# Strassen's algorithm for the up projection of the second MLP, in eight of eleven column groups, on one Trainium2 core

## The chip, the cores and the metric

One core of one Trainium2 chip runs the whole program in one launch. TensorE multiplies matrices into PSUM (eight banks of 128 x 512 float32 are in use here), VectorE and ScalarE do the elementwise work, GpSimd (POOL) issues the DMAs that add into their destination, and SyncE (SP) issues the plain loads. The metric is the device time of one execution in microseconds, lower being better; it is stated as the median of several executions.

## The reference

The program is a decoder trunk of two layers over 512 tokens of width 1024 in float32. Layer 0 is an attention mixer (eight forgetting heads, eight stick-breaking heads), layer 1 a gated short convolution. Behind each mixer comes an MLP with a causal convolution of three taps. Only the second of these MLPs is touched here:

```python
def conv_ffn(h, norm_g, w_up, conv_w, w_down):
    xn = rms_norm(h, norm_g)
    u = causal_dwconv(xn @ w_up, conv_w)
    g, val = u[..., :D_FF], u[..., D_FF:]
    return (jax.nn.silu(g) * val) @ w_down
```

`w_up` is 1024 x 5632 (2816 gate columns, then 2816 value columns), `w_down` 2816 x 1024. The result is added to the residual `h`.

## The kernel before

Activations lie in SBUF feature-major: 128 features on the partitions, 512 tokens along the free axis; `h` is eight such tiles. Every float32 product is made of three TensorE products of rounded halves (high·high, high·low, low·high), so each operand needs a high half, written by ScalarE as a rounded copy, and a low half, written by VectorE as the difference. For the activations these are `hs_hi` and `hs_lo`, taken from `h` times the norm's gain; the norm's own row, one factor per token, is not ready then, so it is multiplied in afterwards, on the way out of PSUM. `Norm.scaled` holds work back until that row (`norm.row`) exists; `Norm.spread` (L311) writes it.

Weights come in chunks of 512 KB or less. `want` lists them in the order of use. `load` (L215) issues the transfer into a `raw` tile on SP's queue, ScalarE makes `whi` (L245), VectorE makes `wlo` (L246), and there are three buffers of each. `weights` hands out the next chunk and has the two behind it loaded and halved (`AHEAD = 2`), so the instructions of a chunk stand on ScalarE's and VectorE's queues two chunks ahead of their use. `want_sum` lists a chunk that is a sum of blocks of the weight matrix: the first block is loaded, the others are added in the same tile by accumulating DMAs on POOL's queue (L230).

Each engine executes its instructions in the order in which the program issues them, and waits there for what an instruction needs. That order is the order of the Python calls; `clock`, `spend` and `after` only delay a few pieces of work (the norm's sums and row) by an estimate of TensorE's time.

The second MLP has two parts:

- `up` (L949): 22 pairs of 128 gate columns and 128 value columns. Each pair has two chunks; `project` makes 24 products of 512 tokens for each, into PSUM tags "a" (2 buffers) and "b" (4). `gate` then runs on each accumulator: times the norm's row (y, L954), the three taps (`causal_conv`: one ScalarE copy at L362, two VectorE taps at L365), SiLU (L958), and `product`.
- the down projection in `mlp_last` (L1025), by Strassen's algorithm: the inner dimension in two halves of 11 feature tiles, the tokens and the output columns in two halves each. `product` (L1048) writes four blocks a, b, c, d of the gated activations (11 tiles of 256 tokens each), and `add_to` (L1042) adds a into b and b into c by SBUF-to-SBUF accumulating DMAs. Seven products p1, q5, p7, p6, p2, p3, q4 of six steps (`GROUPS`) follow. The halves of an operand are made one product ahead into two pairs of tiles; the weight sums are built in the tile `chain` (p1, q5's neighbours and so on, L230); the seven results are joined on VectorE with the residuals, which TensorE has transposed to token-major.

## Time and profile before

| what | us |
|---|---|
| median of three executions | 1190.8 (1190.32 to 1191.4) |
| the profiled execution, whole | 1190.44 |
| the profiled execution, span on the core | 1188.7 |
| the first matmul of the second MLP starts | 827.32 |
| its norm row is usable on VectorE | 839.88 |
| the 13th chunk (of 44) starts | 895.55 |
| the down projection starts | 1074.02 |
| the last matmul | 1184.57 |

The profile is one execution. Its page gives busy time by engine, the span in 40 slices, DMA queues, the chain of work that ended last, the costliest groups of instructions and the DMA issues. A row of a group names line, engine, operation and "out<-in" by the program's tile names, with a count, and then busy time and the mean of one in ns. A row in order of time gives start, duration, engine, line, and in brackets the idle time before it with what ended that. A row of a stretch gives its bounds, its length, and then for TensorE, its weight loads, VectorE, ScalarE and POOL the busy time with the number of instructions, then the granted TensorE clock, the share of time for which the 16 DMA engines were busy, and GB/s. A DMA row gives the median time from issue to landing. The engine PE is TensorE, DVE is VectorE, ACT is ScalarE.

### The profile page before, as it was taken

The page shows a single profiled execution, that of the slowest core. Times are in us where ns is not written, and L with a number is a line of the kernel's source. Part 1 is how long each engine was busy: PE and PEld are TensorE (multiplying, and loading weights), DVE is VectorE, ACT ScalarE, POOL GpSimd, SP SyncE. Part 2 cuts the span into 40 slices and gives each one's busy share as a digit, 9 for nine tenths or more (in the row PEclk, how much of TensorE's full clock was granted, in tenths as well). Part 3 has the DMA queues.
Part 4 walks back from the last instruction along what each step waited for, and adds up shares of the span by engine and source line. Part 5 has one row for each costly group of instructions (what it writes and reads, how often), then busy time and mean ns, then how long its engine had stood idle before and what let it go on. Part 6 is the DMA issues. An engine that isn't in the chain of part 4 may idle for free.

```text
span 1188.7 us, 14686 instructions
## 1 busy us (share of the span) xinstructions
PE 1178.9 (99%) x5711; PEld 958.0 (81%) x5711; DVE 800.2 (67%) x1270; ACT 523.6 (44%) x794; POOL 44.6 (4%) x77
## 2 busy tenths in 40 slices
PE   9999999999999999999999999999999999999998
PEld 7887787888888888888888888888888888888886
DVE  5787898968777777763333555555677666669884
ACT  6556676645444444432222222333343333337552
POOL 3000000000000000000000000000000000014110
PEclk9999999999999999999999999999999999999999
DMA  6312121123333333332333323324543433369781
GB/s 190 102 37 71 54 71 55 54 72 89 89 101 94 89 101 95 89 94 85 96 98 106 89 89 102 93 89 125 167 107 89 123 104 106 105 147 199 159 225 60
DMA packets 189462, 122.14 MB, mean 103 GB/s; under 512 B 5228, under 2 KB 175516, under 8 KB 189392
## 3 DMA queue, kind: packets, MB, share of 16 engines
q1 hardware_dynamic: 182112, 106.94, 30.0%
q0 software_dynamic: 7120, 14.19, 6.9%
q8 instruction: 45, 0.74, 0.3%
q14 instruction: 25, 0.20, 0.0%
q10 hardware_dynamic: 160, 0.07, 0.0%
HBM read 116.59 MB, written 2.10 MB: 100 GB/s over the span
## 4 chain that ended last, share of the span: by engine, by line
PE 93%; DVE 4%; ACT 1%; issue 0%; DVEq 0%; ACTq 0%
PE psb L266 14%; PE psb L268 14%; PE psb L267 14%; PE psa L266 11%; PE psa L268 11%; PE psa L267 11%; PE psb L534 3%; PE psb L535 3%; PE psb L536 3%; PE psb L652 1%; PE psa L748 1%; PE psa L534 1%; PE psa L535 1%; PE psa L536 1%; DVE rest L693 1%; DVE wlo L246 1%
## 5 line engine op out<-in xcount | busy, mean ns | idle before, releaser
L245 ACT ACTIVATE whi<-raw 128x1024 fp32r<-128x1024 f32 (+3 forms) x192 | 200.1, 1043 | 321.4 <-PE psb L267 142.5
L246 DVE TENSOR_TENSOR wlo<-raw,whi 128x1024 fp32r<-128x1024 f32 (+3 forms) x192 | 230.5, 1201 | 90.7 <-ACT whi L245 89.2
L266 PE MATMUL psb<-hs_hi,whi 128*128 128x512 f32 x592 | 237.4, 401 | 0.0
L268 PE MATMUL psb<-hs_hi,wlo 128*128 128x512 f32 x592 | 234.0, 395 | 0.0
L267 PE MATMUL psb<-hs_lo,whi 128*128 128x512 f32 x592 | 232.8, 393 | 0.0
L266 PE MATMUL psa<-hs_hi,whi 128*128 128x512 f32 x432 | 171.5, 397 | 0.6 <-ACT whi L245 0.6
L268 PE MATMUL psa<-hs_hi,wlo 128*128 128x512 f32 x432 | 170.8, 395 | 0.3 <-DVE wlo L246 0.2
L267 PE MATMUL psa<-hs_lo,whi 128*128 128x512 f32 x432 | 170.4, 395 | 0.0
L365 DVE SCALAR_TENSOR_TENSOR u<-y,taps,u 128x510 f32<-128x510 f32 (+1 forms) x176 | 131.0, 747 | 3.2 <-ACT u L362 0.4
L268 PEld LDWEIGHTS psb<-hs_hi,wlo 128*128 128x128 f32 x592 | 111.2, 188 | 26.3
L266 PEld LDWEIGHTS psb<-hs_hi,whi 128*128 128x128 f32 x592 | 111.4, 188 | 24.7 <-issue 1.2
L267 PEld LDWEIGHTS psb<-hs_lo,whi 128*128 128x128 f32 x592 | 111.2, 188 | 24.7
L268 PEld LDWEIGHTS psa<-hs_hi,wlo 128*128 128x128 f32 x432 | 81.2, 188 | 20.2 <-DVE wlo L246 1.1
L266 PEld LDWEIGHTS psa<-hs_hi,whi 128*128 128x128 f32 x432 | 81.2, 188 | 19.3 <-ACT whi L245 0.9
L267 PEld LDWEIGHTS psa<-hs_lo,whi 128*128 128x128 f32 x432 | 81.1, 188 | 19.3 <-DVE hs_lo L825 0.4
L954 DVE TENSOR_TENSOR y<-psb,nrow_n 128x512 f32<-128x512 f32 x44 | 30.4, 691 | 81.6 <-PE psb L268 81.6
L958 ACT ACTIVATE u<-u 128x512 f32<-128x512 f32 x44 | 27.8, 632 | 89.9 <-DVE u L365 89.8
L362 ACT ACTIVATE u<-y,taps 128x512 f32<-128x512 f32 x88 | 63.1, 719 | 1.2 <-DVE y L954 1.1
L534 PE MATMUL psb<-whi,hs_hi 128*128 128x256 f32 (+1 forms) x162 | 54.7, 338 | 0.0
L535 PE MATMUL psb<-wlo,hs_hi 128*128 128x256 f32 (+1 forms) x162 | 53.2, 328 | 0.0
L536 PE MATMUL psb<-whi,hs_lo 128*128 128x256 f32 (+1 forms) x162 | 53.0, 327 | 0.0
L954 DVE TENSOR_TENSOR y<-psa,nrow_n 128x512 f32<-128x512 f32 x44 | 30.4, 690 | 21.8 <-PE psa L268 18.6
(293 smaller groups left out, 1773.8 us busy)
## 6 DMA issues: line engine op xcount, KB each, us to landing
raw<-in_ffn_w_up SPq DMA_DIRECT2D x88, 512.0 KB, 3.7
raw<-in_attn_w_in SPq DMA_DIRECT2D x24, 512.0 KB, 4.0
raw<-in_conv_w_in SPq DMA_DIRECT2D x24, 512.0 KB, 3.8
raw<-in_ffn_w_down SPq DMA_DIRECT2D x21, 512.0 KB, 3.6
chain<-in_ffn_w_down POOLq DMA_DIRECT2D x15, 512.0 KB, 8.0
raw<-in_ffn_w_down SPq DMA_DIRECT2D x16, 448.0 KB, 3.2
raw<-in_attn_w_out SPq DMA_DIRECT2D x8, 512.0 KB, 3.6
raw<-in_conv_w_out SPq DMA_DIRECT2D x8, 512.0 KB, 3.5
```

The lines of the kernel that those rows point to most:

```text
L245: return (act.activation(hi[:, at_], raw[:, at_], AF.Copy), dve.tensor_tensor(lo[:, at_], raw[:, at_], f32(hi[:, at_]), op=ALU.subtract))
L246: dve.tensor_tensor(lo[:, at_], raw[:, at_], f32(hi[:, at_]), op=ALU.subtract))
L266: made = [pe.matmul(acc, w[0], rhs[0], start=first, stop=False), pe.matmul(acc, w[0], rhs[1], start=False, stop=False), pe.matmul(acc, w[1 ...
L267: pe.matmul(acc, w[0], rhs[1], start=False, stop=False),
L268: pe.matmul(acc, w[1], rhs[0], start=False, stop=last)]
L362: act.activation(dst, src, AF.Copy, scale=tap(2))
L365: dve.scalar_tensor_tensor(dst[:, d:], src[:, 0:S - d], tap(j), dst[:, d:], op0=ALU.mult, op1=ALU.add)
L534: pe.matmul(acc, lhs[0], w[0], start=first, stop=False)
L535: pe.matmul(acc, lhs[0], w[1], start=False, stop=False)
L536: pe.matmul(acc, lhs[1], w[0], start=False, stop=last)
L954: dve.tensor_tensor(y, acc, norm.row, op=ALU.mult)
L958: act.activation(u[0], u[0], AF.Silu)
```

## The change

Up to the second MLP nothing moves. In the second MLP:

- **The up projection.** The 22 pairs are taken as 11 groups of two. The first three groups (`CLASSIC = 3`, six pairs, 12 chunks) are made as before. The other eight are 2 x 2 block products: 1024 inner features in two halves, 512 tokens in two halves, and the columns in two halves, namely the group's 256 gate columns and its 256 value columns. Strassen's algorithm in Winograd's form makes the four output blocks from seven products (p1, p7, p3, p6, p2, q5, q4), each with an inner dimension of 512, 256 columns and 256 tokens: 24 matmuls of 256 columns in `seven`.
- **Operands.** `prepare`, called in two halves at j = 0 and j = 2 of the classic pairs, multiplies `h` by gain and norm row, forms the sums and makes the high and low halves of the seven operands (`forms`), which are kept for all groups.
- **Weights of a group.** The blocks (0,0) into X, (0,1) into Y, (1,0) into W and (1,1) into Z are loaded by SP. Sums: (1,1) is added to Y by POOL, X to Y by VectorE, (0,1) to X by POOL, (1,0) to Y by POOL. Halves are taken in between, for p1, p7, p6, p2, q5, q4 and (one group later) p3.
- **PSUM.** A group uses three banks, A, T and R. Products that enter the same output block are summed in one bank; R starts as the negative of A, copied by ScalarE, so that its matmuls add to what is there.
- **`slot(g, s)`** issues the product s of group g and then the other engines' work that stands behind it: the weights of later products, and the joins, taps, SiLU and product of the group before, now 2 x 512 wide on some engines.
- **`Blocks`** keeps the gated activations in one layout of 22 x 512 in three tiles, with a into b added by two POOL DMAs.
- **The last stage.** The order of the products becomes p1, p7, p6, p2, q5, q4, p3; `operand` makes an operand's halves two steps ahead and remakes the blocks in place for the next product; sums of products are built up in the PSUM banks A, T, R, so that fewer joins are left; the chain tiles and buffers are others.
- Pools: `hs_hi` and `hs_lo` become the tiles `hs_a`, `hs_b`; the norm's tiles get a pool `own`; the pool `work` is closed before the second MLP.

```diff
+CLASSIC = 3
...
-    hs_hi = const.tile([P, ND, S], F32R, tag="hs_hi", name="hs_hi")
-    hs_lo = const.tile([P, ND, S], F32R, tag="hs_lo", name="hs_lo")
+    hs_a = hsp.tile([P, 12, S], F32R, tag="hs_a", name="hs_a")
+    hs_b = hsp.tile([P, 4, S], F32R, tag="hs_b", name="hs_b")
...
-    HF, GROUPS, chain = NF // 2, ((0, 2), (2, 2), (4, 2), (6, 2), (8, 2), (10, 1)), []
+    HF, HT = NF // 2, S // 2
+    GROUPS = ((0, 2), (2, 2), (4, 2), (6, 1), (7, 2), (9, 2))
...
-    want_ffn(1)
-    want_last()
+    want_ffn(1, 2 * CLASSIC)
...
+    class Blocks:
...
+        def product(self, j, n, g, u):
...
+            to = self.at(j, n)
+            plus, minus = (LEFT, RIGHT) if j < HF else (RIGHT, LEFT)
+            dve.tensor_tensor(to[:, :, plus], g[:, :, plus], u[:, :, plus], op=ALU.mult)
+            dve.scalar_tensor_tensor(to[:, :, minus], g[:, :, minus], -1.0, u[:, :, minus], op0=ALU.mult, op1=ALU.mult)
+            for k0, k1 in ((0, HEAD), (HEAD, HF)):
+                if j + n == k1:
+                    nc.gpsimd.dma_start(self.block("b", k0, k1 - k0), self.block("a", k0, k1 - k0), accum_op=ALU.add)
+
+    def seven(acc, w, x, fresh, last=True):
+        for i in range(2):
+            to, c = acc[:, i * HT:(i + 1) * HT], slice(i * P, (i + 1) * P)
+            for k in range(4):
+                for t, (a, b) in enumerate(((0, 0), (0, 1), (1, 0))):
+                    pe.matmul(
+                        to, w[a][:, k, c], x[b][:, k, :], start=fresh and i + k + t == 0,
+                        stop=i == 1 and k == 3 and t == 2, skip_group_check=not fresh)
...
+        def prepare(half):
+            k0 = 2 * half
...
+            for x, f in ((x0, k0), (x1, k0 + 4)):
+                for i in range(2):
+                    dve.scalar_tensor_tensor(x[:, i, :], h[:, f + i, :], gain_of(norm.base, f + i), norm.row, op0=ALU.mult, op1=ALU.mult)
...
+            form("p1", x0[:, :, LEFT])
+            dve.tensor_tensor(s0, x0[:, :, LEFT], x0[:, :, RIGHT], op=ALU.subtract)
+            form("p7", s0)
...
+        def load_pair(g):
+            s = st[g] = {}
+            s["X"], s["Y"] = (mp.tile([P, 4, 2 * P], F32, tag=t, name=f"{t}{layer}{g}", bufs=2) for t in "XY")
+            nc.sync.dma_start(s["X"], block_of(g, 0, 0))
+            nc.sync.dma_start(s["Y"], block_of(g, 0, 1))
...
+        def add_block(g, n, kh, half):
+            nc.gpsimd.dma_start(st[g][n], block_of(g, kh, half), accum_op=ALU.add)
...
+        def slot(g, s):
+            on, was, soon = g in groups, g - 1 in groups, g + 1 in groups
+            form, n, fresh = (("p1", "A", True), ("p7", "T", True), ("p3", "R", False), ("p6", "R", False), ("p2", "A", False),
+                              ("q5", "R", False), ("q4", "T", False))[s]
+            if s == 2:
+                if was:
+                    product(g - 1, form, n, fresh)
+            elif on:
+                product(g, form, n, fresh)
+            p, c = g - 1, st.get(g)
+            if s == 0:
+                if was:
+                    weights_of(p, "p3", "Z")
+                    join(p, "yg", st[p]["T"], st[p]["Xs"])
+                if on:
+                    dve.tensor_tensor(c["Y"], c["Y"], c["X"], op=ALU.add)
+                    add_block(g, "X", 0, 1)
+                    load_one(g, "W", 1, 0)
+                if soon:
+                    load_pair(g + 1)
+            elif s == 1:
+                if on:
+                    act.activation(bank_of(g, "R"), c["A"], AF.Copy, scale=-1.0)
+                    weights_of(g, "p6", "Y")
+                if soon:
+                    add_block(g + 1, "Y", 1, 1)
+                if was:
+                    conv(p, 0, 0)
+            elif s == 2:
+                if on:
+                    kept(g, "P7s", c["T"])
+                    add_block(g, "Y", 1, 0)
+                    weights_of(g, "p2", "W")
+                if was:
+                    conv(p, 0, 1)
+            elif s == 3:
+                if was:
+                    to_wide(p, "yv", LEFT, st[p]["R"])
+                if on:
+                    weights_of(g, "q5", "X")
+                if was:
+                    act.activation(wides[p]["ug"], wides[p]["ug"], AF.Silu)
+                    conv(p, 1, 0)
+            elif s == 4:
+                if on:
+                    kept(g, "Xs", c["R"])
+                    weights_of(g, "q4", "Y")
+                if was:
+                    conv(p, 1, 1)
+            elif s == 5:
+                if was:
+                    blocks.product(2 * p, 2, wides[p]["ug"], wides[p]["uv"])
+                if on:
+                    load_one(g, "Z", 1, 1)
+                    open_wides(g)
+                    to_wide(g, "yg", LEFT, c["A"])
+                if soon:
+                    weights_of(g + 1, "p1", "X")
+            else:
+                if on:
+                    join(g, "yv", c["R"], c["P7s"])
+                if soon:
+                    weights_of(g + 1, "p7", "Y")
...
+            if j == 0:
+                norm.scaled(lambda: prepare(0))
+            if j == 2:
+                norm.scaled(lambda: prepare(1))
+            if j == 2 * CLASSIC - 2:
+                load_pair(base)
+                add_block(base, "Y", 1, 1)
...
+        PHASES = ("p1", "p7", "p6", "p2", "q5", "q4", "p3")
...
+        def operand(i):
...
+            halves_to(t[:, 0, 0:nk, :], t[:, 1, 0:nk, :], blocks.block(name, k0, nk), sign)
+            a, b, c, d = (blocks.block(n, k0, nk) for n in "abcd") if p in (1, 2, 3) else (None,) * 4
+            if p == 1:
+                dve.tensor_tensor(b, b, c, op=ALU.add)
+            elif p == 2:
+                dve.tensor_tensor(a, b, a, op=ALU.subtract)
+            elif p == 3:
+                dve.tensor_tensor(b, b, d, op=ALU.add)
...
+        A, T, R = ([] for _ in range(3))
+        home = {"p1": (A, "a", True), "p7": (T, "b", True), "p6": (R, "b", False), "p2": (A, None, False), "q5": (R, None, False),
+                "p3": (R, None, False), "q4": (T, None, False)}
```

More of the change, by code (lines that the diff above doesn't have):

```diff
@@ L283, in __init__ @@
             self.row, self.held = None, []
-            self.acc = work.tile([P, S], F32, tag="y", name=f"nacc_{name}") if name != "n0" else None
+            self.acc = own.tile([P, S], F32, tag="nrow", name=f"nacc_{name}", bufs=1) if name != "n0" else None
         def feed(self, f, src):
@@ L311, in spread @@
         def spread(self):
-            self.row = work.tile([P, S], F32, tag="nrow", name=f"nrow_{self.name}", bufs=1)
+            self.row = own.tile([P, S], F32, tag="nrow", name=f"nrow_{self.name}", bufs=1)
             t = bank("c")
@@ L397, in trunk, with want_ffn @@
     want_out_last()
-    def want_ffn(layer):
-        for j in range(NF):
+    def want_ffn(layer, pairs=NF):
+        for j in range(pairs):
             want(ffn_w_up[layer], 0, 8, j * P, P)
@@ L521, in values @@
                 w = ws[k // 4]
[L522 removed]
+                mm3_rhs(acc[:, 0:n], [t[:, tok] for t in hs(k)], (w[0][:, k % 4, :], w[1][:, k % 4, :]), k == 0, k == ND - 1)
                 spend(0.33)
```

327 lines of the change are left out of this document (214 added, 113 removed).

## The prediction

> **What bounds the kernel now.** I read the page's first two parts and the chain of work, then busy time by stretches, then order of time on single engines.
>
> ```profile
> span 1188.7 us, 14686 instructions
> PE 1178.9 (99%) x5711; PEld 958.0 (81%) x5711; DVE 800.2 (67%) x1270; ACT 523.6 (44%) x794; POOL 44.6 (4%) x77
> PEclk9999999999999999999999999999999999999999
> PE 93%; DVE 4%; ACT 1%; issue 0%; DVEq 0%; ACTq 0%
> ```
>
> TensorE is busy throughout, at full clock, and carries 93% of the chain. The stretches of the second MLP (columns: us, then each engine's busy time with its count, clock, DMA share, GB/s):
>
> ```profile
> 900.00:922.33 22.33, 22.33 (x98) 18.06 (x97) 15.72 (x23) 8.88 (x13) 0.00 (x0) 1.00 0.33 95
> 839.80:895.50 55.70, 55.70 (x241) 45.02 (x240) 40.79 (x58) 23.19 (x33) 0.95 (x1) 1.00 0.40 113
> 895.50:1074.00 178.50, 178.50 (x769) 144.23 (x769) 123.79 (x172) 69.26 (x92) 9.51 (x9) 1.00 0.44 112
> 1074.00:1188.70 114.70, 110.96 (x495) 89.72 (x493) 86.44 (x114) 59.60 (x82) 21.89 (x19) 0.99 0.70 162
> ```
>
> The 178.5 us hold 768 matmuls of 512 columns, eight groups of 96 (the edges count one or two more): 232.5 ns each, 22.3 us a group, no gap. A weight chunk (24) takes 5.58 us. VectorE is busy 69% here, so it has room that the change can use up.
>
> The profiled execution took 1190.4 us, its span plus 1.7; the median of the three runs is 1190.8, so the sum below stands for both. About 0.2% (2.4 us) is what a measurement of this kernel can tell from no change.
>
> **Part 1: TensorE's work.** A group becomes seven products of 24 matmuls, 168 of 256 columns. The kernel has such matmuls in the attention values; here 13 in a row from 72.85 on:
>
> ```profile
> 72.85 0.28 PE L535 MATMUL psb<-wlo,hs_hi 128*128 128x256 f32 x1
> ...
> 74.39 0.28 PE L536 MATMUL psb<-whi,hs_lo 128*128 128x256 f32 x1
> ```
>
> 13 steps in 1.54 us: 118 ns start to start, weight loads hidden. A product is 2.83 us, a group 19.8 instead of 22.3. If TensorE stayed the bound, eight groups would save 20 us.
>
> **Part 2: the first six pairs (still classic) carry the preparation.** Each half of prepare puts on VectorE 4 scalings, 4 sums and 7 low halves, all 512 wide. Prices:
>
> ```profile
> 839.88 0.69 DVE L954 TENSOR_TENSOR y<-psa,nrow_n 128x512 f32<-128x512 f32 x1 [2.18 <-ACT nrow_n L316]
> 840.49 0.68 DVE L954 TENSOR_TENSOR y<-psb,nrow_n 128x512 f32<-128x512 f32 x1
> 841.09 1.22 DVE L246 TENSOR_TENSOR wlo<-raw,whi 128x1024 fp32r<-128x1024 f32 x1
> 842.22 2.73 DVE L365 SCALAR_TENSOR_TENSOR u<-y,taps,u 128x511 f32<-128x511 f32 x4
> 850.92 0.39 PE L266 MATMUL psa<-hs_hi,whi 128*128 128x512 f32 x1
> ```
>
> Start to start, instructions overlap a little: 512 wide 0.61 us, weights' low half 1.13, tap 0.68. The norm row arrives at 839.9; the fifth chunk's product is due at 850.92. As the changed kernel is built, that chunk's low half stands behind 4 scalings (0.68), 11 operations of 0.61, both y (0.61), 4 taps (0.68) and itself (1.22 to its end): 2.7+6.7+1.2+2.7+1.2 = 14.5, so 854.5. TensorE waits 3.6 us where it waited none. From there to the ninth chunk's low half stand the second half of prepare (2.7+6.7), 4 low halves (4.5), 4 y (2.4), 7 taps (4.8) and 4 products of 256 (0.42 by the row below, some 0.34 start to start: 1.4), 22.5 us, against 4 x 5.58 = 22.3 of TensorE. In ScalarE's order the ninth chunk's high half, which waits until TensorE frees a buffer, stands ahead of prepare's high halves, so VectorE waits there about 1.7: TensorE waits 1.9 more. Sum +5.5; between 3.6 (the second hidden) and 8 (every high half waited for). Then VectorE has 13 us of work in 22, and the backlog is gone before the first Strassen product.
>
> ```profile
> L1052 DVE TENSOR_TENSOR blk_a<-u,u 128x256 f32<-128x256 f32 x11 | 4.7, 426 | 0.4
> L362 ACT ACTIVATE u<-y,taps 128x512 f32<-128x512 f32 x88 | 63.1, 719 | 1.2 <-DVE y L954 1.1
> L316 ACT ACTIVATE nrow_n<-psc 128x512 f32<-128x512 f32 x3 | 1.8, 598 | 12.0 <-PE psc L315 12.0
> raw<-in_ffn_w_up SPq DMA_DIRECT2D x88, 512.0 KB, 3.7
> ```
>
> On SP's queue the last classic chunk's load now stands behind the first X and Y loads, which wait for prepare to let go of their buffers (about 876); it lands 3.7 later, at 880, wanted at 884: 0. The operands also take prepare's results from h, so the norm's row is waited for no longer than by the first y.
>
> The Trainium skill ("TensorE: Matmul & The Clock Gate", Part 1) has TensorE's clock halve after an idle window of about 3.4 us. The first wait is about that long; by that rule up to 1.7 us would be added. No gap of this trace tests it (clock 1.00 in every stretch), and the sum goes without.
>
> **Part 3: the loop of the Strassen groups.** ScalarE's load per group (7 high halves of 1.06, 5 copies of PSUM of 0.6, 4 tap copies of 0.72, one SiLU of about 1) is 14.3 us: cover enough. VectorE: 7 low halves and Y+X (8 x 1.13), 8 taps (5.4), 2 joins and 2 products of 512 (4 x 0.61) = 16.9 us of 19.8. That alone fits. But its order is fixed, and one wait lies in it. p6's low half must be done with Y before POOL may add the fourth block to Y; when that lands, ScalarE makes q4's high half, VectorE its low half, and everything of VectorE behind that (the next p1, p7, p6) queues. From q4's low half to the end of p6's, VectorE runs: five of 1.13 (q4, p1, p7, Y+X, p3), four taps (2.7), two products and two joins (2.4), p6 1.22: 12.0. Around it:
>
> ```profile
> 1063.94 1.23 DVE L246 TENSOR_TENSOR wlo<-chain,whi 128x1024 fp32r<-128x1024 f32 x1 [0.17 <-ACT whi L245]
> 1065.47 1.20 POOL L230 DMA_DIRECT2D chain<-in_ffn_w_down x1 [0.44 <-DVE wlo L246]
> 1103.41 0.90 POOL L230 DMA_DIRECT2D chain<-in_ffn_w_down x1 [0.74 <-DVE wlo L246]
> 816.10 1.06 ACT L245 ACTIVATE whi<-raw 128x1024 fp32r<-128x1024 f32 x1 [3.38 <-PE psb L267]
> ```
>
> 0.3 us from the low half's end (1065.17) to the add's issue, then the landing L, then about 0.1 and 1.06 on ScalarE. So a group takes 13.5 + L, if that is over 19.8: the loop leaves TensorE's bound at L = 6.3. L of single adds of 512 KB, by stretches about one issue each (1122:1124 nothing near it; 1052:1054 one load beside it; 1063:1065 an add 3 us before; 1065:1067 its second row, an add 1.6 us before):
>
> ```profile
> chain<-in_ffn_w_down POOLq DMA_DIRECT2D x1, 512.0 KB, 5.8
> ...
> raw<-in_ffn_w_down POOLq DMA_DIRECT2D x1, 512.0 KB, 6.5
> ...
> raw<-in_ffn_w_down POOLq DMA_DIRECT2D x1, 512.0 KB, 7.1
> chain<-in_ffn_w_down POOLq DMA_DIRECT2D x1, 512.0 KB, 8.0
> ```
>
> Those have 256 pieces of 2 KB; the new blocks have 512 of 1 KB. POOL's instruction took 0.90 for 128 pieces and 1.20 for 256, so 0.6 more. In the loop X's add is issued 4.9 us before Y's, and the load of Z runs beside it: between the 6.5 and the 7.1, 6.8, plus 0.6 is L = 7.4. Ends: 5.8+0.6 = 6.4 and 8.0+0.6+0.7 (the second load) = 9.3. Then a group takes 20.9; TensorE waits 1.1 us at q4, and saves 1.4 a group, not 2.5.
>
> The first group has no p3 and no backlog: 6 products and the next p1 (19.8), p6's halves (1.06+1.22), 0.3+L+1.16, so q4's low half of the second group starts 23.6+L = 31.0 after the first product. Six more rounds of 20.9 are 125.4; then q4's low half, a tap, an operand, two products and the down projection's first low half, 4.9. Two adds inside SBUF for the blocks stand in POOL's queue ahead of X's and Y's once each: 1.5. Sum 162.8 for what took 178.5: -15.7.
>
> What else queues there: POOL issues the next group's (1,1) add ahead of X's. It waits for Y's load, issued after q4's low half (1.3 into the round) and landed 3.7 later, so it is out at 5.1, before X's add can go (7.4). X's add lands at 14.8; q5's halves and three taps behind it end at 19, before Y's landing at 12.4+7.4 = 19.8. Only if X took 2 us more would it be late next.
>
> **Part 4: the last stage.** Its 462 matmuls stay 512 wide. Added: the last group's p3, 24 x 118 ns = +2.8. VectorE's work from the first to the seventh step (18 us: operands, p3's halves, joins and taps of the last group) equals TensorE's 18.2, so it costs at most 0.5. POOL's queue is the risk: q5's adds stand ahead of p6's, nine whole blocks from the stage's start.
>
> ```profile
> 1120.00:1140.00 20.00, 20.00 (x88) 16.22 (x87) 16.24 (x21) 12.27 (x17) 6.95 (x6) 1.00 0.86 146
> ```
>
> Those 20 us at a DMA share of 0.86 hold five adds of 512 KB, one of half that and one load: 17.2 us of all 16 engines. The stretch from 900 has four loads at 0.33 of 22.33, so 1.8 a load, and an add takes 15.4/5.5 = 2.8. Nine are 25.2, two loads among them 3.7, and p6's own first block 5.8: it lands some 34.7 us in, wanted at 32.7: +2 (nothing, if the loads come later; 6, if POOL's waits hold two adds up). With the 0.5, +2.5. The joins that go away, by the sums in PSUM, lay beside TensorE: 0. The tail behind the last matmul is the same.
>
> **Sum:** 5.5 - 15.7 + 2.8 + 2.5 = -4.9: 1185.5 us.
>
> **Rivals.**
> TensorE stays the bound (adds land within 6.3 us): 55 products x 2.83 = 155.7 instead of 162.8, so -4.9-7.1 = -12: 1178.4. For it: 5.8 alone. Against: 7.1 with an add before it, and smaller pieces. The Trainium skill's fit ("DMA: Bandwidth & Descriptors", Anatomy of one DMA), 2.0 us plus bytes over 436 GB/s, gives 3.2 us for 512 KB as an estimate, generation being small, and would bring this case; the trace disagrees, with 5.8 at best.
>
> The add's wait decides against the change: L at its upper end, 9.3, makes a group 22.8, longer than the classic 22.3, and the sum 7 x 1.9 = 13.3 worse: +8.4, 1198.8. Place: q4's low half on VectorE. It decides from L = 8.1 on, where the sum is 0. For it: 8.0 median of the chain's adds, three adds and four loads a group; against: the adds are 5 to 7 us apart, and the 8.0 belong to adds closer than 3.
>
> Narrow matmuls don't keep 118 ns over whole stages, so the change doesn't do what it says: at 133 a group costs 22.3 as before. Against: the row above. At 133 throughout, with parts 2 and 4: +8, 1198.
>
> **How the numbers follow.** Forecast 48%, TensorE-bound 15%, late adds 33%, slow narrow matmuls 4%. The forecast's own range, L from 6.5 to 8.1, is 1179 to 1190. Faster by over 0.2% is L under 7.75: 33 of the 48, and the 15: 0.48. Within 0.2%: 13 of the 48, 2 of the late: 0.15. Slower: 0.37. The range to 80%: 1177 (TensorE-bound, less of part 4) to 1201 (late adds, and 2 us of parts 2 and 4).
>
> **What would show it.** Narrow matmuls 118 ns apart within a product. A wait of 3 to 4 us of TensorE at the fifth chunk, on VectorE's wlo. In each group, a wait of about 1 us at q4's first low-half matmul, on VectorE's wlo, which waited for ScalarE's whi, which waited for the DMA into Y; the period 20.9; Y's add landing 7.4 after its issue. If VectorE shows no wait at q4, the TensorE-bound case holds; if TensorE waits over 2.5 us a group, the late adds do. If TensorE waits at another product, or VectorE's instructions are longer than before, part 3 is wrong in its mechanism.

## The result and the profile after

The changed kernel takes 1198.62 us (median; 1197.68 to 1203.78) against 1190.67 for the kernel before: a ratio of 1.0075, 95% interval 1.0056 to 1.0094. It is slower by 0.75%, where 1185.5 was forecast. Its executions spread over 6 us, those of the kernel before over 1.1.

From the page of the changed kernel:

```profile
span 1195.9 us, 16031 instructions
PE 1169.0 (98%) x6287; PEld 978.8 (82%) x6287; DVE 831.0 (69%) x1292; ACT 572.6 (48%) x859; POOL 74.8 (6%) x98
...
PEclk9999999999999999999999999999999999989999
...
PE 84%; DVE 8%; DMA 5%; ACT 2%; issue 1%; SPq 0%; DVEq 0%; ACTq 0%; POOL 0%; POOLq 0%
```

TensorE is busy 9.9 us less than before. The smaller products alone promise some 17 (20 in the groups, less 2.8 for the last group's p3); the half clock, told of below, takes back 5.4 of them. The span is even 7.2 us longer: TensorE's share of the chain fell from 93% to 84%, DMA appears with 5%. By stretches (classic pairs, Strassen groups, last stage; then three single groups; columns as in the prediction):

```profile
828.80:900.07 71.27, 69.78 (x309) 56.26 (x308) 62.60 (x102) 33.13 (x47) 3.62 (x3) 1.00 0.45 119
900.07:1075.77 175.70, 162.78 (x1321) 162.06 (x1320) 133.88 (x159) 104.41 (x134) 33.91 (x27) 0.96 0.87 185
1075.77:1195.90 120.13, 114.53 (x512) 91.75 (x510) 91.28 (x123) 67.11 (x95) 24.36 (x21) 1.00 0.69 158
...
937.24:964.21 26.97, 21.56 (x170) 21.35 (x169) 17.74 (x21) 13.24 (x17) 4.32 (x4) 0.94 0.86 165
1008.07:1028.13 20.06, 20.06 (x170) 20.02 (x169) 17.09 (x21) 13.48 (x17) 3.48 (x3) 1.00 0.86 184
1048.09:1075.77 27.68, 22.48 (x170) 22.28 (x169) 18.58 (x23) 15.11 (x21) 6.19 (x5) 0.88 0.92 227
```

Against the stretches of before, the classic pairs take 3.0 us more (71.27 for 68.23, from 827.32 to 895.55), the groups 2.8 less (175.70 for 178.5) and the last stage 5.4 more (120.13 for 114.7). About 1.0 us of the 3.0 is work that only changed its place: eight transposes, which the kernel before makes in its last stage, stand among the classic pairs as built. The second MLP starts 1.5 us later (828.80 for 827.32), though nothing ahead of it was changed.

Four of the eight groups take 19.9 to 20.1 us and the first, which has no p3, 17.1, all with TensorE never idle. The other three have a wait each: 5.7, 2.6 and 5.5 us, counted from the start of one matmul to the start of the next. The first of them, on TensorE and then on ScalarE:

```profile
951.32 0.28 PE L1065 MATMUL psa<-p_hi,wlo_p 128*128 128x256 f32 x1
957.01 0.58 PE L1065 MATMUL psb<-q_hi,whi_q 128*128 128x256 f32 x1 [5.41 <-ACT Xs L1160]
```

```profile
951.10 1.06 ACT L1017 ACTIVATE whi_q<-X 128x1024 fp32r<-128x1024 f32 x1 [5.56 <-DMA X<-in_ffn_w_up]
952.06 0.58 ACT L1152 ACTIVATE yv<-psb 128x512 f32<-128x512 f32 x1
952.68 1.33 ACT L370 ACTIVATE uv<-yv,taps 128x512 f32<-128x512 f32 x2
955.42 1.06 ACT L1017 ACTIVATE whi_q<-Y 128x1024 fp32r<-128x1024 f32 x1 [1.41 <-DMA Y<-in_ffn_w_up]
956.38 0.58 ACT L1160 ACTIVATE Xs<-psb 128x512 f32<-128x512 f32 x1
```

The product that waits is q5. It adds to bank R, and before it may, ScalarE must copy R out (Xs). An engine's order was said above to be that of the Python calls. Here it is not: the text of `slot` has Xs ahead of q4's high half, but as built Xs stands behind it on ScalarE, and q4's high half waits for the fourth block's landing in Y. So that landing holds up q5, one product earlier than the prediction had it. X's own add is late here too: its high half starts at 951.10, so q5 would have waited nearly 2 us in any case (1.8 in the run with Xs first, below). What landed when, from single issues of the changed kernel (the add inside SBUF; X's add beside it; Y's fourth block in an undisturbed group; the last group's, with two of the last stage's loads):

```profile
head<-head POOLq DMA_DIRECT2D x1, 896.0 KB, 9.6
...
X<-in_ffn_w_up POOLq DMA_DIRECT2D x1, 512.0 KB, 12.2
...
Y<-in_ffn_w_up POOLq DMA_DIRECT2D x1, 512.0 KB, 6.0
...
p_hi_chain<-in_ffn_w_down SPq DMA_DIRECT2D x1, 512.0 KB, 10.6
Y<-in_ffn_w_up POOLq DMA_DIRECT2D x1, 512.0 KB, 11.7
p_lo_chain<-in_ffn_w_down SPq DMA_DIRECT2D x1, 512.0 KB, 12.3
```

Behind each of the three waits TensorE ran at half its clock (narrow matmuls 213 ns apart instead of 118), for 3.2, 3.4 and 5.1 us:

```profile
957.01:960.20 3.19, 3.19 (x15) 3.19 (x16) 3.16 (x5) 1.39 (x2) 0.00 (x0) 0.50 0.40 111
1001.00:1004.40 3.40, 3.40 (x18) 3.40 (x18) 3.37 (x5) 1.14 (x2) 0.00 (x0) 0.52 0.52 148
1067.71:1072.80 5.09, 5.09 (x24) 5.09 (x25) 4.32 (x6) 3.24 (x6) 0.94 (x2) 0.50 1.04 196
```

That costs 1.5, 1.6 and 2.3 us: 5.4 in all, beside 13.4 of waits (what is left when the matmuls' usual distance is taken off).

### The profile page after: what moved, and what is told of

Its sections match the earlier page's. It is cut to its first block, busy times and chain, and to the rows that moved or that the text cites. A ratio compares the mean times of both kernels' runs of the same rounds, so it can differ in the third digit from the quotient of the medians.

```text
span 1195.9 us, 16031 instructions
## 1 busy us (share of the span) xinstructions
PE 1169.0 (98%) x6287; PEld 978.8 (82%) x6287; DVE 831.0 (69%) x1292; ACT 572.6 (48%) x859; POOL 74.8 (6%) x98
## 4 chain that ended last, share of the span: by engine, by line
PE 84%; DVE 8%; DMA 5%; ACT 2%; issue 1%; SPq 0%; DVEq 0%; ACTq 0%; POOL 0%; POOLq 0%
PE psb L270 11%; PE psb L272 11%; PE psb L271 11%; PE psa L272 8%; PE psb L1065 8%; PE psa L271 8%; PE psa L270 8%; PE psb L1371 4%; PE psa L1065 3%; PE psa L1371 2%; DMA Y<-in_ffn_w_up 2%; PE psb L641 1%; PE psa L737 1%; DMA q_hi_chain<-in_ffn_w_down 1%; DVE wlo L250 1%
## 5 line engine op out<-in xcount | busy, mean ns | idle before, releaser
L270 PE MATMUL psb<-hs_a,whi 128*128 128x512 f32 x464 | 186.4, 402 | 0.0
L272 PE MATMUL psb<-hs_a,wlo 128*128 128x512 f32 x464 | 184.1, 397 | 0.0
L272 PE MATMUL psa<-hs_a,wlo 128*128 128x512 f32 x304 | 121.2, 399 | 1.7 <-DVE wlo L250 1.6
L270 PE MATMUL psa<-hs_a,whi 128*128 128x512 f32 x304 | 120.2, 395 | 1.3 <-ACT whi L249 1.3
L270 PEld LDWEIGHTS psb<-hs_a,whi 128*128 128x128 f32 x464 | 87.6, 189 | 19.9 <-issue 1.2
L272 PEld LDWEIGHTS psb<-hs_a,wlo 128*128 128x128 f32 x464 | 87.1, 188 | 20.1
L271 PE MATMUL psb<-hs_b,whi 128*128 128x512 f32 x232 | 91.7, 395 | 0.0
L271 PE MATMUL psb<-hs_a,whi 128*128 128x512 f32 x232 | 91.7, 395 | 0.0
L1371 PE MATMUL psb<-whi,act 128*128 128x512 f32 x220 | 70.5, 398 | 0.7 <-ACT whi L249 0.6
L373 DVE SCALAR_TENSOR_TENSOR u<-y,taps,u 128x511 f32<-128x511 f32 (+1 forms) x88 | 65.5, 748 | 1.8 <-ACT u L370 0.4
L271 PE MATMUL psa<-hs_b,whi 128*128 128x512 f32 x152 | 60.2, 396 | 0.0
L271 PE MATMUL psa<-hs_a,whi 128*128 128x512 f32 x152 | 60.1, 396 | 0.0
L1065 PE MATMUL psb<-q_hi,whi_q 128*128 128x256 f32 x128 | 39.1, 305 | 12.9 <-ACT Xs L1160 12.9
```

What stands on the lines that cost most here:

```text
L270: made = [pe.matmul(acc, w[0], rhs[0], start=first, stop=False), pe.matmul(acc, w[0], rhs[1], start=False, stop=False), pe.matmul(acc, w[1 ...
L271: pe.matmul(acc, w[0], rhs[1], start=False, stop=False),
L272: pe.matmul(acc, w[1], rhs[0], start=False, stop=last)]
L373: dve.scalar_tensor_tensor(dst[:, d:], src[:, 0:S - d], tap(j), dst[:, d:], op0=ALU.mult, op1=ALU.add)
L1065: pe.matmul(to, w[a][:, k, c], x[b][:, k, :], start=fresh and i + k + t == 0, stop=i == 1 and k == 3 and t == 2, skip_group_check=not fresh)
L1371: pe.matmul(acc[tb], acts[i][:, a, k, tok], w[b][:, k, :], start=fresh and k0 + k + t == 0, stop=k0 + k == HF - 1 and t == 2, skip_group_c ...
```

## The experiments

Every run is compared with the kernel before on the same chip; "the changed kernel" is 1198.6 throughout.

### Where the long waits come from

**The add of a to b moved from POOL's transfers to VectorE.**

```diff
-                if j + n == k1:
-                    nc.gpsimd.dma_start(self.block("b", k0, k1 - k0), self.block("a", k0, k1 - k0), accum_op=ALU.add)
+            if HEAD <= j + n <= HF:
+                k0 = 0 if j + n == HEAD else j
+                b, a = self.block("b", k0, j + n - k0), self.block("a", k0, j + n - k0)
+                dve.tensor_tensor(b, b, a, op=ALU.add)
```

> VectorE adds block a to block b (one addition of 1792 columns in the fourth Strassen group's time, then up to 512 columns a group) in place of the two adding transfers inside SBUF. Theory (shared DMA): the first two long waits of TensorE at q5 (5.7 and 2.6 us) come from these two transfers, beside which the adds into X and Y land 9 to 12 us after their issue where they take 6 to 8 otherwise. Then both waits go, with the 1.5 and 1.6 us of half clock behind them, and only the last group's wait stays: about 10.9 us less than the changed kernel, 1187.5. Rival (the loop is at its edge and lands late by chance): waits of the same sum remain in the loop, 1196 to 1202.

Measured: 1196.31 us, ratio 1.0050 (1.0035 to 1.0065). The two waits shrank from 5.7 and 2.6 to 1.0 and 1.3 us, but others of 3.5 and 1.9 came in groups that had none, and the last group's stayed (5.9). Sum and time are the rival's, nearly; but the waits at the two places that the theory named shrank by 6.0 us, which chance alone doesn't explain. Two things changed at once here: the transfers went, and VectorE got more work.

**The same add left out**, to part the transfers from VectorE's added work.

> The changed kernel without the two transfers that add block a to block b inside SBUF, and with nothing in their place: this part of the computation is left out. It parts the two things that e1 changed together, the transfers taken away and the work put on VectorE. If e1's new waits (3.5 us in the fourth Strassen group, 1.3 and 1.9 us in two others) came from the loop of 13.5 + L itself, which the first long wait had hidden by giving the adds a head start, they are here too: 3 to 6 us of waits in the loop ahead of the last group, 1194 to 1197. If they came from VectorE's added work, no group but the last waits more than 0.5 us: 1187 to 1189.

Measured: 1191.78 us, ratio 1.0008 (0.9999 to 1.0018), so the two transfers cost 6.8 us of the changed kernel. The time lies between the two ranges that were named. Waits of 0.6, 2.1 and 1.5 us remain ahead of the last group; the 3.5 us of the run before is gone, so it came of VectorE's added work. The remaining ones follow the reckoned loop of 13.5 + L. Six groups of this run together, then two of them alone, and the landings of the fourth block in these two:

```profile
916.98:1040.79 123.81, 120.52 (x1010) 119.85 (x1009) 103.74 (x125) 79.96 (x102) 21.83 (x17) 1.00 0.83 179
...
977.48:999.47 21.99, 20.21 (x170) 20.01 (x169) 17.31 (x21) 13.24 (x17) 4.70 (x4) 1.00 0.78 168
1020.84:1040.79 19.95, 19.95 (x170) 19.95 (x169) 17.37 (x21) 13.36 (x17) 2.77 (x3) 1.00 0.85 185
```

```profile
Y<-in_ffn_w_up POOLq DMA_DIRECT2D x1, 512.0 KB, 7.8
...
Y<-in_ffn_w_up POOLq DMA_DIRECT2D x1, 512.0 KB, 6.0
```

With L = 7.8 the loop gives 21.3, measured 22.0; with 6.0 it gives 19.5, and TensorE's 19.95 bounds. Over the six L averages 6.8, which gives 20.3; they took 123.81/6 = 20.6.

**One more such transfer.**

```diff
+        spare = mp.tile([P, 4, HT], F32, tag="spare", name="spare_sum")
+        pool.memset(spare, 0.0)
...
+                    if g == 8:
+                        nc.gpsimd.dma_start(spare, blocks.block("c", 0, 4), accum_op=ALU.add)
```

> One more adding transfer inside SBUF (512 KB, from block c into a tile that nothing reads) is issued on POOL's queue in group 8's slot q5, a group whose successor shows no wait; the output is the same. Shared DMA: in the group after it the adds into X and Y land 2 to 5 us later, and q5 there waits 2 to 3 us, with some 1.6 us of half clock behind: 4 us longer than the changed kernel, about 1202. Rival (chance): no wait comes in at that place, within 1 us of the changed kernel.

Measured: 1199.91 us, ratio 1.0082 (1.0067 to 1.0097). A wait of 1.6 us came in at the named place (2 to 3 were expected), with no half clock behind it; but one of 1.5 came also a group earlier, and the time lies within the changed kernel's spread. The direction fits, and alone it would settle nothing.

**The last group: the last stage's loads held back.**

```diff
                 if fresh:
-                    nc.sync.dma_start(v, src)
+                    issued = nc.sync.dma_start(v, src)
+                    if i >= held_from[0] + 4:
+                        tc.add_manual_dep(issued.ins, gate_at[NF // 2 - 1].ins.name, mybir.DependencyInfo(
+                            mybir.DependencyClass.Sync, mybir.DependencyReason.DATA), reason="hold")
```

> The loads of the last stage, from its fifth chunk on, are held back until ScalarE makes the last Strassen group's q4 high half. Shared DMA: the last group's wait at q5 (5.2 us, with 2.2 us of half clock) comes from the seven loads that SP issues into freed buffers beside the last adds; it falls under 1 us. The first sums of the last stage then land later and give back 0 to 3 us: 1191.5 to 1195. Rival: the add into Y is late for another reason (it is 4.6 us behind X's on POOL's queue), and the wait stays at 4 us or more: 1197 or longer.

Measured: 1202.64 us, ratio 1.0107 (1.0092 to 1.0122). The last group's wait is gone altogether, and its fourth block lands after 6.1 us, so the loads beside it were the cause:

```profile
Y<-in_ffn_w_up POOLq DMA_DIRECT2D x1, 512.0 KB, 6.1
```

But the last stage now waits 3.0 us at 1089 and 7.3 at 1107, each with half clock behind: the held loads were needed. Right on the cause, wrong on the price of the cure.

**The order on ScalarE.**

```diff
-                    kept(g, "Xs", c["R"])
-                    weights_of(g, "q4", "Y")
+                    copied = kept(g, "Xs", c["R"])
+                    behind(weights_of(g, "q4", "Y"), copied)
```

> ScalarE's copy Xs of bank R (which must be taken before q5 adds to that bank) is put ahead of q4's high half in ScalarE's order; nothing else changes. Theory (order on ScalarE): q5 waits because Xs stands behind q4's high half, which waits for the fourth block's add into Y. With Xs first q5 waits only for X's halves, and the add into Y has one product (2.8 us) more: of the three waits (5.7, 2.6, 5.5 us, with 5.3 us of half clock) some 1 us at q5 of the first and 1 to 2 us at q4 of the first and third remain: 1185 to 1188. Rival (q5 waits for its own weights): the waits stay within 1 us, 1197 to 1201.

Measured: 1197.44 us, ratio 1.0061 (1.0044 to 1.0077): 1.2 less, where the changed kernel's own executions spread over 6. The three waits shrank (5.7 to 1.8, 2.6 to none), but q5 waited in other groups (3.2, 1.9, 1.0 us): Xs still stands behind X's high half and three copies, and X's add now went out 0.8 to 1.9 us behind the next group's add into Y (2.2 to 3.7 before) and took 8.4 to 10.6 us, and most of the last group's wait only moved to q4 (2.4 and 1.0 us there, 1.3 left at q5). The order says which product waits, not how long the landings take.

### Taking the landing out of the loop

**The fourth block added by VectorE.** It is the block (1,0), which lies in SBUF as W.

```diff
-                    add_block(g, "Y", 1, 0)
                     weights_of(g, "p2", "W")
+                    dve.tensor_tensor(c["Y"], c["Y"], c["W"], op=ALU.add)
```

> The fourth block of a group, which POOL added to Y by a transfer, is already in SBUF as W: VectorE adds W to Y instead (1.1 us a group), so no landing lies any more between p6's low half and q4's high half. The adds inside SBUF stay. Theory (loop with a landing in it): the waits in the loop were this landing L, in the loop that the prediction reckoned at 13.5 + L a group, made longer by whatever else the DMA engines did. Then no group waits more than 1 us at q5 or q4, the half-clock stretches go, and eight groups take about 157 us: 1198.6 - 13.0 - 5.3 = 1180.5, between 1179 and 1184. Rival (the landing into X is the next limit): q5 waits 1 to 3 us in two or more groups on X's halves, 1185 to 1190. Rival (VectorE becomes the bound at 18.0 us of 19.8): waits on VectorE's low halves in every group, 1186 or more.

Measured: 1189.56 us, ratio 0.9994 (0.9985 to 1.0004), 9 us less than the changed kernel and 9 more than expected. Groups, then last stage, of this run:

```profile
899.89:1062.21 162.32, 159.32 (x1321) 158.43 (x1320) 140.18 (x165) 103.69 (x134) 23.15 (x19) 0.99 0.73 169
1062.21:1188.10 125.89, 117.24 (x512) 93.69 (x510) 92.93 (x125) 66.82 (x95) 24.85 (x22) 0.97 0.69 158
```

The groups gave 13.4 us of the 18 or so that were expected: q5 still waited 2.35 us, with half clock behind, and 0.7 and 0.8 us in two other groups. There X's landing came late, and Xs stands behind X's high half on ScalarE, with four more instructions between. The time lies in the first rival's range, but only in part for its reason: the last stage took back 5.8 (125.89 for 120.13). In it p6 now waits for a weight sum:

```profile
1101.00 0.49 PE L1371 MATMUL psb<-whi,act 128*128 128x512 f32 x1 [4.13 <-ACT whi L249]
1102.26 0.79 PE L1371 MATMUL psb<-wlo,act 128*128 128x512 f32 x1 [0.76 <-DVE wlo L250]
```

The shorter loop brings the stage forward, but not its sums: those start when buffers come free and then take their time on the DMA engines.

**Both adds on VectorE.** The edits of the first run and of the one above together.

> As the run before, and block a is added to b by VectorE too, so that of POOL's transfers in a group only the second and the third block's adds are left. Shared DMA: X's adds land within 6 to 7.5 us in every group, and the time is that of the run before or up to 2 us less: 1179 to 1182. VectorE as the bound: in the groups with the added 1.9 or 0.6 us TensorE waits by about that, 2 to 4 us more than the run before.

Measured: 1193.02 us, ratio 1.0023 (1.0013 to 1.0033): 3.5 us more than the run before, as the second case had it. VectorE, with some 17.6 of 20 us a group (141.11 over eight in a row below), has little room. The large addition stands in its order ahead of Y+X, and behind it Y+X began 3.5 us later than in the run before (940.00 for 936.52), and with it X's add:

```profile
932.79 2.02 DVE L1058 TENSOR_TENSOR head<-head 128x1792 f32<-128x1792 f32 x1
```

So the wait at that q5 stayed (2.55 us), though the transfer beside it was gone, and the last group waited 2.8.

**The preparation one pair later**, on top of the fourth block's edit.

```diff
-            if j == 0:
+            if j == 1:
                 norm.scaled(lambda: prepare(0))
-            if j == 2:
+            if j == 3:
                 norm.scaled(lambda: prepare(1))
```

> As the first run of this call, with the two halves of the operands' preparation put one classic pair later (j = 1 and j = 3 for 0 and 2). The wait of 1.65 us at the fifth chunk (and 0.5 at the ninth) is taken to be VectorE's queue of preparation work right behind the norm's row. Then these waits go or fall under 0.5 us together, and 1 to 2 us less than the first run of this call is measured, 1179. Rival: the same work is late one pair later, or the first Strassen products wait for their weights, whose tiles the preparation lets go later: a wait of 1 to 4 us at the seventh to the 13th chunk, 1180 to 1184.

Measured: 1188.68 us, ratio 0.9983 (0.9973 to 0.9992). The waits of 1.65 and 0.5 us are gone, as expected, and the first Strassen product starts 3.0 us earlier (896.89 for 899.89; 1.0 of it is the eight transposes, back in the last stage). Only 0.9 arrived at the end:

```profile
896.89:1062.92 166.03, 160.13 (x1321) 159.28 (x1320) 140.77 (x167) 104.09 (x135) 24.14 (x19) 0.98 0.73 165
```

The groups took 3.7 us more (166.03 for 162.32): the wait of 2.35 us at q5 grew to 4.5, and the half clock behind it lasted twice as long. X's add went out 2.3 us earlier there but took 12.1 us, for 10.7 in the run before; why is not shown. The last stage took 1.9 less (123.98 for 125.89), still with a wait of 4.4 us ahead of p6.

### The order of POOL's transfers

**q5's adds behind p6's**, on top of the run above.

```diff
+                    adds[i] = nc.gpsimd.dma_start(v, src, accum_op=ALU.add)
+                    if i in after_add:
+                        behind(adds[i], adds[after_add[i]])
...
+        for g in range(6):
+            after_add[at_first + 6 * PHASES.index("q5") + g] = at_first + 6 * PHASES.index("p6") + 5
```

> As e7, and in the last stage q5's six adds are put behind p6's last add on POOL's queue; before, four to six of them stood ahead of p6's adds, which are wanted 31 us earlier. Theory (order of POOL's queue): the wait of 4.4 us at p6's first steps (1097.5 in e7) and the 2 us of half clock behind it come from this order, and they are why the last stage grew when the loop ahead of it became shorter. Then the wait falls under 1 us, and 5 to 6 us less than e7 is measured: 1183. Rival (the DMA engines themselves are the limit there: 12 sums are wanted within 31 us whatever their order): the wait stays at 3 us or more, or moves to p7 or q5, 1187 to 1190.

Measured: 1184.70 us, ratio 0.9955 (0.9940 to 0.9970), 4.0 less (5 to 6 were expected). POOL's queue of the run before, where X, Y and two of the p tiles are q5's sums, and then of this one:

```profile
1079.62 1.20 POOL L234 DMA_DIRECT2D q_hi_chain<-in_ffn_w_down  x1 [3.32 <-DMA q_hi_chain<-in_ffn_w_down]
1080.35 2.64 POOL L234 DMA_DIRECT2D Y_chain<-in_ffn_w_down  x2
...
1093.84 1.20 POOL L234 DMA_DIRECT2D q_lo_chain<-in_ffn_w_down  x1 [0.77 <-DVE wlo L250]
```

```profile
1092.48 1.20 POOL L235 DMA_DIRECT2D q_lo_chain<-in_ffn_w_down  x1 [0.93 <-DVE wlo L253]
1093.21 2.95 POOL L235 DMA_DIRECT2D X_chain<-in_ffn_w_down  x2
```

The wait at p6 is gone. 2.4 us came instead at p2, whose plain loads took 8 to 11 us beside the twelve adds that now went out together.

**Xs first, and the add of a to b in smaller pieces**, on top of that.

```diff
-            for k0, k1 in ((0, HEAD), (HEAD, HF)):
+            for k0, k1 in ((0, 6), (6, HEAD), (HEAD, HF)):
```

> As e8, with Xs ahead of q4's high half on ScalarE, and the adding transfer of block a into b cut so that its first six tiles go right behind the classic pairs and one tile later. Theory: with the large transfer out of the second Strassen group's time X's add there lands in about 7 us, and q5 waits for its own operands alone; the waits of 4.5 and 1.2 us in the loop fall under 1 us together, with 2 us of half clock: 5 to 7 us less than e8, 1176 to 1179. Rival: the first Strassen group, which has three adds of its own, takes the wait over, 1180 to 1183.

Measured: 1186.51 us, ratio 0.9967 (0.9954 to 0.9979): 1.8 us more, a miss. The large add's wait moved a group forward (2.6 us), and waits of 0.6 to 1.5 us stand in five others, where the run before had two. X and Y were loaded 2 to 4 us later, counted from the group's first product, and their two adds went out closer together and landed later. That q4's halves, now behind Xs, let go of Y later is the likely reason; it was not tried apart.

**What is wanted first goes first**, on the last kernel but one (without Xs first and the smaller pieces).

```diff
-                    add_block(g + 1, "Y", 1, 1)
+                    behind(add_block(g + 1, "Y", 1, 1), c["added"])
...
+                    if i in after_low:
+                        tc.add_manual_dep(adds[i].ins, lows[after_low[i]].ins.name, mybir.DependencyInfo(
+                            mybir.DependencyClass.Sync, mybir.DependencyReason.DATA), reason="hold")
...
+        for g in range(6):
+            after_low[at_first + 6 * PHASES.index("q4") + g] = at_first + 6 * PHASES.index("p2") + 4
```

`c["added"]` is X's add of the group, `lows` the instructions that make the low halves.

> As e8, with two orders of transfers more: X's add of a group stands ahead of the next group's first add into Y on POOL's queue, and q4's six adds wait until VectorE has made the low half of p2's fifth chunk. Theory (what is wanted first is to have the DMA engines first): X's add lands in 6 to 6.5 us instead of 8, the waits of 1.0 and 0.6 us at q5 in later groups go, the 3.7 us in the second one shrink to 1 to 3; and p2's loads land in 4 to 6 us instead of 8 to 11, so its 2.4 us of waits go: 3 to 6 us less than e8, 1179 to 1182. Rival: the adds are then late in their turn (p7's low half in the loop, q4 in the last stage), and the time is e8's, 1184 to 1187.

Measured: 1174.75 us (1174.22 to 1174.88), ratio 0.9862 (0.9847 to 0.9877): 10 us less than the run it builds on, and 1.4% faster than the kernel before. The three stretches and the page's chain:

```profile
828.80:897.18 68.38, 68.38 (x301) 55.49 (x300) 61.23 (x101) 32.45 (x46) 1.39 (x1) 1.00 0.42 116
897.18:1054.13 156.95, 156.95 (x1321) 156.86 (x1320) 141.11 (x167) 104.88 (x135) 24.87 (x19) 1.00 0.78 179
1054.13:1172.40 118.27, 114.59 (x520) 92.44 (x518) 92.59 (x125) 66.84 (x95) 25.67 (x22) 1.00 0.75 167
```

```profile
PE 92%; DVE 5%; ACT 1%; issue 1%; DMA 0%; DVEq 0%; SPq 0%; ACTq 0%
```

No wait at all is left in the groups, and they take 156.95 us: TensorE's own time, at full clock. The adds inside SBUF are still there, 896 KB and all; with slack in the loop they cost nothing. The expected 3 to 6 us were too few: the longest wait went whole, and some 2.7 us of half clock with it. Against the run it builds on, the groups gave 8.0 us (156.95 for 164.94) and the last stage 2.6 (118.27 for 120.83); the two orders were not run apart.

**The same orders on the changed kernel alone**: fourth block on POOL, preparation as it was.

> The orders of transfers of e11 (X's add ahead of the next group's first add into Y; in the last stage q5's adds behind p6's, q4's adds held until p2's fifth chunk) on the changed kernel as it was: the fourth block is still added to Y by POOL, and the preparation lies where it lay. It tells whether the orders alone are enough. Theory (loop of 13.5 + L with the fourth block's landing in it): with two adds issued just ahead of it that landing takes 7.5 to 9 us, a group 21 to 22.5 us instead of 19.95, and q5 waits 1 to 2.5 us in most groups; the last stage's waits go all the same: 1188 to 1196. Rival (the orders do it all): no group waits over 0.5 us, and the time is e11's with the preparation's 2 to 3 us on top, 1177 to 1179.

Measured: 1224.37 us, ratio 1.0283 (1.0265 to 1.0302). The group from 973.71 waits so at its q5, and the fourth blocks' landings of three groups in a row (the second is this one's):

```profile
991.74 0.58 PE L1071 MATMUL psb<-q_hi,whi_q 128*128 128x256 f32 x1 [3.63 <-ACT Xs L1166]
```

```profile
Y<-in_ffn_w_up POOLq DMA_DIRECT2D x1, 512.0 KB, 9.9
...
Y<-in_ffn_w_up POOLq DMA_DIRECT2D x1, 512.0 KB, 10.5
...
Y<-in_ffn_w_up POOLq DMA_DIRECT2D x1, 512.0 KB, 10.8
```

```profile
947.84:1077.55 129.71, 110.47 (x843) 109.45 (x841) 87.59 (x103) 66.81 (x85) 20.72 (x16) 0.89 0.71 150
```

Five groups in 129.71 us, 25.9 each, every one with a wait at q5 and half clock behind it. The loop theory had the direction; the landing was 10.5 rather than its 7.5 to 9, with two adds sent out just ahead of the fourth block. 13.5 + 10.5 gives 24.0; the 1.9 us above it are about what the half clock cost behind the three waits of the changed kernel. The last stage shows no wait here; but behind so slow a loop its sums also have more time, so this alone does not show that its orders work by themselves. Whether the fourth block passes over the DMA engines or over VectorE decides the rest: 50 us between the two last runs (some 2 of them the preparation's).

## Why the prediction was wrong

**Part 1, TensorE's work: right.** 118 ns held over whole stages; the run without waits takes 156.95 us for the 155.7 forecast.

**Part 2, the classic pairs: right in mechanism and place, too dear.** The classic stretch lost 2.0 us for 5.5, beside the 1.0 of the eight transposes. The fifth chunk's low half came late, as reckoned:

```profile
853.42 1.03 PE L1323 MATMUL psc<-ident,h 128*128 128x128 f32 x8
855.84 0.50 PE L272 MATMUL psa<-hs_a,wlo 128*128 128x512 f32 x1 [1.38 <-DVE wlo L250]
```

TensorE wanted it at 852.97, two matmuls into the chunk, and got it at 855.84. But the built order has two of the sixth chunk's products and eight of the last stage's transposes in that gap, so that only 1.65 us passed between two matmuls' starts. The second wait measured 0.5 for 1.9. With the preparation one pair later both went.

**Part 3, the loop: the step that failed.** -15.7 was forecast, -2.8 measured. Its equation held within 0.7 us where the clock stayed full: a group takes 13.5 + L where that exceeds TensorE's time. L in the five groups without a wait was 5.9 to 6.6, against the 7.4 taken: POOL's instruction took 1.28 us for a block in 512 pieces, hardly more than the 1.20 for 256, where 0.6 had been added for them. In the other three L was 11.9, 8.7 and 11.7. Three things were wrong:

- "Two adds inside SBUF for the blocks stand in POOL's queue ahead of X's and Y's once each: 1.5." They were priced as places in a queue. They are transfers. X's add, sent out while 896 KB moved for 9.6 us, took 12.2; Y's, sent out as they landed and with X's still under way, 11.9. Leaving both transfers out saved 6.8 us.
- The last group's fourth block was given the same L. Beside it ran seven loads of the last stage, which SP issues as soon as buffers come free; it landed after 11.7, and q5 waited 5.5 us. No step had priced that; holding the loads back removed the wait.
- The half clock was named and left out of the sum. It cost 5.4 us. The Trainium skill ("TensorE: Matmul & The Clock Gate", Part 1) puts it behind an idle window of about 3.4 us. Here 2.3 us of idling (the wait of 2.58) brought it, so the measurement decides.

In us, against the forecast for the groups: 6.3 more of waits (13.4 for 7.1), 5.4 of half clock, 1.3 of TensorE's own: 13.0 for the 12.9 missing.

The place was wrong by one product as well: q5 through Xs on ScalarE, not q4's low half on VectorE, an order that could be read from the built kernel. Setting it right alone was worth 1.2 us. The prediction itself named a wait at another product as the sign that part 3 is wrong in its mechanism, and so it is.

**Part 4, the last stage: right in sum.** +5.3 was forecast, +5.4 measured: 2.85 for p3 and some 2.7 of waits, less 1.0 for the transposes made earlier. Of the 0.9 that is left the run without waits has 0.7 too (118.27 for 114.70, 2.85 of it p3); it is not explained. The first wait is at p6 at 1109.7, behind q5's adds on POOL's queue, at the place and nearly at the price forecast (2.0 for +2). That this queue would also take back 5.8 of the 13.4 us that the loop gained was not foreseen: it came out only when the loop got faster.

**The rivals.** The late adds' 1198.8 is the time that came, by another road: not L = 9.3 in every group, but 11.9, 8.7 and 11.7 in three of eight, and half clock. That the two numbers agree is luck. Its mechanism exists: with L near 10.5 in every group the kernel is slower by 2.8%. The Trainium skill's fit for one DMA ("DMA: Bandwidth & Descriptors", Anatomy of one DMA) gives 3.2 us for 512 KB as an estimate. The adds do not bear it out: 6.0 in the quiet row above, 12.2 beside another. The TensorE-bound case is what the kernel becomes once the fourth block no longer travels and the orders are set.

**Not explained.** In all thirteen profiles with the new tiles the second MLP starts between 827.95 and 828.80, against 827.32 in the one profile of before. About 1 us of it gathers bit by bit between 252 and 828 us, in work whose order is unchanged. No run tests it.

## What to carry to other kernels

A transfer put on a queue is not a place in that queue: price it by what else is in flight on the same DMA engines while it lands, and look above all at the edges of a loop, where the next stage's loads start the moment buffers come free. If a landing lies in a loop that one in-order engine closes, first ask whether the data is already in SBUF; then order the transfers by when they are wanted. And a gain inside a stage arrives at the end only if what the next stage waits for starts earlier too.

## What was unexpected of the hardware

The clock followed quite short waits, and it did so in steps. In every profile the granted clock changes only at moments that lie whole multiples of 3.41 us apart, and where it falls to half it stays there for 3.41, 6.83 or, once, 10.24 us. What counted in the groups was TensorE's idle time within one such step, not the length of a wait: steps at full clock with up to 1.75 us of it were followed by full clock, those with 1.97 or more by half. The second wait of the changed kernel, with the step behind it; the one of 2.35 us in the run with the fourth block on VectorE; and one of 2.05 us in the run without the block adds, which fell across two steps and cost no clock:

```profile
997.72:1001.13 3.41, 1.11 (x10) 0.90 (x9) 2.49 (x4) 2.09 (x4) 0.00 (x0) 1.00 0.68 205
1001.13:1004.55 3.42, 3.42 (x19) 3.42 (x18) 3.38 (x5) 1.01 (x2) 0.00 (x0) 0.50 0.53 152
...
951.46:954.87 3.41, 1.44 (x12) 1.44 (x13) 3.41 (x5) 3.36 (x5) 0.00 (x0) 1.00 0.50 154
954.87:958.28 3.41, 3.41 (x19) 3.41 (x18) 3.27 (x5) 0.68 (x1) 0.00 (x0) 0.50 0.48 154
...
989.98:993.39 3.41, 1.93 (x17) 1.72 (x15) 2.40 (x5) 2.02 (x4) 0.00 (x0) 1.00 0.93 293
993.39:996.80 3.41, 3.12 (x26) 3.12 (x27) 3.38 (x5) 1.76 (x4) 0.00 (x0) 1.00 0.34 106
```

A step at half clock that itself held 0.8 us of idling or more was followed by another one. A matmul's end is modelled, so the bound between 1.75 and 1.97 is no sharper than that; in the last stage of the run without the block adds a step with 1.5 us of idling by the profile was followed by half clock too. So a wait of 2.05 us cost nothing more here and one of 2.35 did, by the way they lay to the steps. The wait of 2.58 made its group 4.0 us longer (23.99 for 19.96). The changed kernel's executions spread over 6 us, those of the version without waits over 0.7; that waits at this edge are the reason is likely and not shown.
